# Plain float32 products for the inputs of a state-space stage

## The chip, the cores and the metric

The kernel runs on one core of one Trainium2 chip. Its time is the device time of one execution in microseconds. TensorE (PE) multiplies, PEld is its loading of the stationary operand, VectorE (DVE), ScalarE (ACT) and GpSimd (POOL) work on tiles, and SyncE (SP) issues nearly all transfers.

## The reference

Two layers of a backbone over 512 latent and 256 context tokens of width 1024, all in float32. Layer 0 has a matrix-memory mixer, layer 1 the state-space mixer (Mamba-2, two directions); a mixer of 16384 experts stands behind each. The change concerns the first line of the state-space mixer's preparation, once for the context and once for the latent tokens:

```python
def prep(h):
    z, xbc, dt_raw = jnp.split(h @ w_in, [B_DI, B_DI + B_CONV_CH], axis=-1)   # 1024 x 6208
    xbc = jax.nn.silu(dw_conv(xbc, conv_w, conv_b))
    xs, bm, cm = jnp.split(xbc, [B_DI, B_DI + B_GROUPS * B_STATE], axis=-1)
    dt = softplus(dt_raw + dt_bias)
    ...
```

`w_in` has 2048 columns for the gate z, 2048 for x, 1024 for B, 1024 for C and 64 for dt. Behind it come a convolution over 5 tokens with SiLU, the chunked scan in both directions (chunks of 128 tokens, 32 heads in 8 groups), a gated norm and the output product. The context's state is where the latent scan starts; the context's own output is not needed, since the layer is the last.

## The kernel before

**Products.** TensorE takes a stationary operand of 128 x 128 and a moving one of 128 x up to 512. Most large products of the kernel are made of exact parts: a float32 number is split in hi (a cast to the type float32r) and lo (the rest, again float32r), and `mm3` (L207 to L210) adds three products in PSUM: hi x hi, hi x lo, lo x hi. One "product" below is such a group of three on the same k (128 rows of the contraction) and the same 128 output channels or tokens.

**Weights.** `raw2` (L149) has SP fetch two k of a weight block in one transfer of 128 x 2 x 512 (512 KB) into one of three `raw` tiles. `wpair` (L165) splits each k: ACT casts it to `whi` (L173), DVE subtracts to get `wlo` (L175), with three tiles of each. A block of weights is 8 k x 512 columns.

**The stage.** `ssd_ctx_in` scales the context, transposes it and splits it (`cinh`, `cinl`); this is done within the expert mixer of layer 0, ahead of the stage. `ssd_ctx` multiplies it with six blocks (B twice, x four times): 32 products of 256 columns each. Behind a block come, for each of four channel groups, the convolution (`conv_silu`: pad L399 and cva L401 on ACT, four cva L403 on DVE, tanh L404 on ACT, st L405 on DVE), transposes (L1142), and for x the state updates (`upd_state`: wx and S L1147 on ACT, a product L1155 on PE, S L1161 on DVE). In the middle, `ssd_in` makes the latent input (`inh`, `inl`, L308 to L313 and L185, L186). `dt_prep` (L1097) multiplies by the 64 dt columns, with its weights split too (w8h, w8l).

`ssd_lat` has 12 latent blocks of 32 products of 512 columns: B and C for four groups, x and z (z with tokens as output rows, `tok_block`), then B and C for the other four, with the scan woven in:

```python
weave(scan(0), project_xz(1))
weave(scan(1), project_bc(1), project_xz(2))
weave(scan(2), project_xz(3))
weave(scan(3), itertools.islice(first, DK))    # the output product's first 12 k
```

A scan has 8 steps (4 chunks x 2 groups). A step fetches the decay sums as a broadcast tile `bcs` of 512 KB (L1313, two buffers), works on it on DVE (L1317, L1319, L1326, L1327) and ACT (L1320, L1325), multiplies states (L1331, L1332, PE), multiplies the weights with x (L1343, four products on PE), and sums on DVE (L1338 to L1346).

**What sets the order.** The code above is only the order of writing. When the kernel is built, a scheduler with its own timing model orders the instructions of each engine; on the chip each engine's queue then runs in that fixed order, and an instruction that waits holds all that stands behind it on its engine. SP's transfers are such a queue as well.

## Time and profile before

| | |
|---|---|
| runs | 5936.06, 5928.29, 5920.93 us; median 5928.29 |
| profiled execution | 5929.8 us, its span 5928.0 us |
| PE | 5272.5 us busy, 89%, 25708 products |
| PEld | 4330.6 us, 73% |
| DVE | 4623.1 us, 78% |
| ACT | 2508.2 us, 42% |
| POOL | 1517.6 us, 26% |
| granted TensorE clock, mean | 0.937 |

Busy time is the union of an engine's instructions. A product's record runs from its start until its last result is out, so records of products that follow each other overlap; what a product occupies is read from one start to the next. The granted clock is the share of 2.4 GHz that TensorE had; its two levels are 1.2 and 2.4 GHz, so 0.91 is a mean over time at either. A plain float32 product with both operands float32 has two records, each with a weight load of its own.

### The profile page before, as it was taken

What the parts mean: (1) busy time and instruction counts of PE and PEld (TensorE: products, weight loads), DVE (VectorE), ACT (ScalarE), POOL (GpSimd) and SP (SyncE); (2) the same over time, 40 slices, a digit from 0 to 9 for tenths busy, and PEclk for the clock granted to TensorE, in tenths of its full rate; (3) what the DMA queues carried; (4) which work ended last, traced back from release to release, by engine and by line L of the source; (5) the groups of instructions that cost most, each with busy time, mean ns of one, the idle gap of its engine ahead of it and who ended that gap; (6) DMA issues with size and microseconds to landing.
All of it is one profiled execution on the core that took longest, in us unless ns stands there. A gap on an engine that the chain in (4) does not pass through costs nothing.

```text
span 5928.0 us, 76907 instructions
## 1 busy us (share of the span) xinstructions
PE 5272.5 (89%) x25708; PEld 4330.6 (73%) x25708; DVE 4623.1 (78%) x8960; ACT 2508.2 (42%) x5186; POOL 1517.6 (26%) x1284
## 2 busy tenths in 40 slices
PE   6899999999997875998699999788877998799998
PEld 4688777766663444898578899667666898688997
DVE  6743567877676788999888889767776998788888
ACT  4643454322222333344333333477874344333333
POOL 1300001345544445121033444000001011133442
PEclk8999999999998887998799999899888998799999
DMA  6765555898879987566698999433334357798996
GB/s 211 240 191 156 161 164 163 282 333 303 301 248 320 327 313 254 168 198 213 207 340 315 347 336 332 155 97 96 104 110 125 121 180 250 254 339 321 345 339 234
DMA packets 655799, 1406.96 MB, mean 237 GB/s; under 512 B 62760, under 2 KB 237496, under 8 KB 650920
## 3 DMA queue, kind: packets, MB, share of 16 engines
q1 hardware_dynamic: 507944, 865.11, 44.1%
q0 software_dynamic: 147456, 536.94, 25.7%
q8 instruction: 201, 3.29, 0.2%
q14 instruction: 198, 1.62, 0.1%
HBM read 1278.10 MB, written 123.70 MB: 236 GB/s over the span
## 4 chain that ended last, share of the span: by engine, by line
PE 40%; DVE 13%; DMA 13%; issue 6%; ACT 4%; POOL 1%; DVEq 0%; SPq 0%; ACTq 0%; POOLq 0%
PE mm L208 6%; PE mm L209 6%; PE mm L210 6%; PE sm L210 4%; PE sm L208 4%; PE sm L209 4%; DMA g<-in_v_dram,idv 4%; DMA g<-in_u_dram,idx 3%; DVE wlo L175 2%; DMA bcs<-acD 2%; PE mx L1032 2%; PE mx L210 1%; PE mx L208 1%; PE mx L209 1%; DMA raw<-in_v_dram 1%
## 5 line engine op out<-in xcount | busy, mean ns | idle before, releaser
L173 ACT CAST whi<-raw 128x512 fp32r<-128x512 f32 x2032 | 1227.0, 619 | 1815.4 <-PE mm L209 575.7
L175 DVE TENSOR_TENSOR wlo<-raw,whi 128x512 fp32r<-128x512 f32 x1979 | 1348.3, 695 | 499.8 <-ACT whi L173 488.0
L860 POOL DMA_INDIRECT g<-in_u_dram,idx x512 | 623.4, 1218 | 1465.8 <-PE mx L210 418.0
L860 POOL DMA_INDIRECT g<-in_v_dram,idv x512 | 679.3, 1327 | 888.0 <-DVE acc L878 316.8
L878 DVE SCALAR_TENSOR_TENSOR acc<-g,act,acc 128x1024 f32<-128x1024 f32 x508 | 655.7, 1291 | 156.2 <-DMA g<-in_v_dram,idv 153.6
L867 DVE CUSTOM_DVE_ANT_0 g<-g,xb 128x1024 f32<-128x1024 f32 x512 | 622.4, 1220 | 161.8 <-DMA g<-in_u_dram,idx 160.6
L210 PE MATMUL sm<-pinh,wlo 128*128 128x384 f32 x2048 | 693.1, 342 | 14.8 <-DVE wlo L175 14.2
L208 PE MATMUL sm<-pinh,whi 128*128 128x384 f32 x2048 | 697.1, 340 | 4.3 <-ACT w L977 3.0
L209 PE MATMUL sm<-pinl,whi 128*128 128x384 f32 x2048 | 694.2, 339 | 0.0
L209 PE MATMUL mm<-wlo,wh 128*128 128x512 f32 x1024 | 400.6, 394 | 11.1 <-DVE wlo L175 11.0
L210 PEld LDWEIGHTS sm<-pinh,wlo 128*128 128x128 f32 x2048 | 386.0, 189 | 23.2 <-DVE wlo L175 22.5
L210 PE MATMUL mm<-whi,wl 128*128 128x512 f32 x1024 | 393.8, 391 | 3.2 <-DVE wl L186 3.2
L208 PEld LDWEIGHTS sm<-pinh,whi 128*128 128x128 f32 x2048 | 386.5, 189 | 12.6 <-ACT w L977 5.6
L208 PE MATMUL mm<-whi,wh 128*128 128x512 f32 x1024 | 362.5, 396 | 35.0 <-ACT wh L185 31.0
L209 PEld LDWEIGHTS sm<-pinl,whi 128*128 128x128 f32 x2048 | 386.6, 189 | 5.5
L209 PE MATMUL mm<-xcl,whi 128*128 128x256 f32 (+1 forms) x1024 | 349.2, 346 | 8.9 <-DVE xcl L186 8.9
L210 PE MATMUL mm<-xch,wlo 128*128 128x256 f32 (+1 forms) x1024 | 332.0, 349 | 21.6 <-DVE wlo L175 21.4
L208 PE MATMUL mm<-xch,whi 128*128 128x256 f32 (+1 forms) x1024 | 344.3, 349 | 5.1 <-ACT xch L185 4.0
L208 PE MATMUL mm<-inh,whi 128*128 128x512 f32 (+1 forms) x768 | 285.8, 376 | 11.1 <-ACT cva L401 6.9
L1057 DVE TENSOR_TENSOR w<-w,gtb 128x384 f32<-128x384 f32 x256 | 232.5, 912 | 63.8 <-DMA gtb<-gD 28.6
L209 PE MATMUL mm<-inl,whi 128*128 128x512 f32 (+1 forms) x768 | 279.9, 366 | 0.0
L1032 PE MATMUL mx<-og,oa 128*128 128x128 f16 x1536 | 199.2, 297 | 86.3 <-DVE og L1027 86.2
(478 smaller groups left out, 10947.3 us busy)
## 6 DMA issues: line engine op xcount, KB each, us to landing
raw<-in_uT_dram SPq DMA_DIRECT2D x256, 512.0 KB
raw<-in_v_dram SPq DMA_DIRECT2D x256, 512.0 KB
raw<-in_w_qk_dram SPq DMA_DIRECT2D x128, 512.0 KB
raw<-in_ada_w_dram SPq DMA_DIRECT2D x96, 512.0 KB
raw<-in_w_up_dram SPq DMA_DIRECT2D x96, 512.0 KB
gD<-sg SPq DMA_DIRECT2D x48, 1024.0 KB
gtb<-gD SPq DMA_DIRECT2D x32, 1536.0 KB
raw<-in_s_in_dram SPq DMA_DIRECT2D x72, 512.0 KB
```

Source lines behind the costliest of these rows:

```text
L173: nc.scalar.copy(hi, raw[:, u])
L175: (eng or next(los["eng"])).tensor_tensor(lo, raw[:, u], hi.bitcast(F32), OP.subtract)
L208: nc.tensor.matmul(o, sh, mh, start=start, stop=False)
L209: nc.tensor.matmul(o, sh, ml, start=False, stop=False)
L210: last["pe"] = nc.tensor.matmul(o, sl, mh, start=False, stop=stop)
L860: d = nc.gpsimd.indirect_dma_start(out=g_, out_offset=None, in_=tab, in_offset=bass.IndirectOffsetOnAxis(ap=ix[:, k:k + 1], axis=0))
L867: nc.vector.tensor_tensor_reduce(out=g_, in0=g_, in1=xb, scale=1.0, scalar=0.0, op0=OP.mult, op1=OP.add, accum_out=act[:, k:k + 1])
L878: nc.vector.scalar_tensor_tensor(acc, g_, act[:, k:k + 1], acc, OP.mult, OP.add)
L1032: nc.tensor.matmul(g4[:, k * P:(k + 1) * P], oa[:, f, :, k], og[:, u, :, k], start=u == 0, stop=u == 1)
L1057: nc.vector.tensor_tensor(w, w, gt[0][:, :, j], OP.mult)
```

## The change

The inputs are no longer split. `ssd_ctx_in` and `ssd_in` write one float32 tile each (`cinx`, `inx`), `parts` copies instead of splitting where no lo tile is given, `dt_prep` uses its weights as fetched, and `ch_block` and `tok_block` multiply the fetched weights (`wraws`, the raw tile itself) with it in one plain float32 product in place of three.

```diff
+    def wraws(wt, n, kc):
+
+        for k in range(0, kc, 2):
+            raw = raw2(wt[n, k:k + 2].rearrange("k p c -> p k c"))
+            for u in range(2):
+                yield raw[:, u]
+                tick()
...
+    def parts(hi, lo, s, src):
+
+        if lo is None:
+            nc.scalar.copy(hi[s], src)
+        else:
+            split(hi[s], lo[s], src)
...
+    def ch_whole(o, wt, n, kc, x):
+
+        T = o[0].shape[1]
+        pair = T == CTX
+        for k, w in enumerate(wraws(wt, n, kc)):
+            for c in range(4):
+                last["pe"] = nc.tensor.matmul(o[c], w[:, c * P:(c + 1) * P], x[:, k, :T], start=k == 0 and not pair,
+                                              stop=k == kc - 1 and not (pair and c % 2 == 0))
+            yield
...
-        for _ in ch_steps(o, wt, n, kc, xh, xl, eng):
+        for _ in ch_whole(o, wt, n, kc, xh) if xl is None else ch_steps(o, wt, n, kc, xh, xl, eng):
...
+        if xl is None:
+            for k, w in enumerate(wraws(wt, n, kc)):
+                for t, x in enumerate(o):
+                    last["pe"] = nc.tensor.matmul(x, xh[:, k, t * P:(t + 1) * P], w, start=k == 0, stop=k == kc - 1)
+            return o
...
-                split(xh[s], xl[s], o.rearrange("p (c t) -> p c t", c=4))
+                parts(xh, xl, s, o.rearrange("p (c t) -> p c t", c=4))
...
-            w8h = wq.tile([P, 8, 64], F32R, name="w8h")
-            w8l = wq.tile([P, 8, 64], F32R, name="w8l")
-            split(w8h, w8l, w8)
             for k in range(8):
-                mm3(o[:64, :nt * P], w8h[:, k], w8l[:, k], inh[:, k, :nt * P], inl[:, k, :nt * P], k == 0, k == 7)
+                nc.tensor.matmul(o[:64, :nt * P], w8[:, k], x_in[:, k, :nt * P], start=k == 0, stop=k == 7)
...
-        inh = pool.tile([P, 8, T], F32R, name="inh")
-        inl = pool.tile([P, 8, T], F32R, name="inl")
+        x_in = pool.tile([P, 8, T], F32, name="inx")
...
-        inh = cinp.tile([P, 8, CTX], F32R, tag="cinh", name="cinh", bufs=1)
-        inl = hcp.tile([P, 8, CTX], F32R, tag="h_ctx", name="cinl", bufs=1)
+        x_in = cinp.tile([P, 8, CTX], F32, tag="cinh", name="cinx", bufs=1)
...
-                for c, o in enumerate(ch_block(A["s_in"], 4 + n, 8, inh, inl, T)):
+                for c, o in enumerate(ch_block(A["s_in"], 4 + n, 8, x_in, None, T)):
...
-                for t, o in enumerate(tok_block(A["s_in"], n, 8, inh, inl, T)):
+                for t, o in enumerate(tok_block(A["s_in"], n, 8, x_in, None, T)):
```

The scheduler orders the instructions anew from the context input's transposes on; ahead of these the order is the same on every engine. On POOL nothing moves.

On ACT, in the context part at the first x block, before the change (xst is the transposed x, pad, cva and st the convolution, wx the x scaled by dt, whi the casts):

```order
L1147 ACTIVATE wx<-xst,dt_wst_32170 128x64 x12
L173 CAST whi<-raw 128x512
L404 ACTIVATE st<-cva 128x256
L401 ACTIVATE cva<-mm,c_scb,c_scw 128x256
L399 COPY pad<-mm 128x256
L173 CAST whi<-raw 128x512
L1233 COPY xst<-sm 128x2x128
L173 CAST whi<-raw 128x512
L401 ACTIVATE cva<-mm,c_scb,c_scw 128x256
L173 CAST whi<-raw 128x512
L1233 COPY xst<-sm 128x2x128
```

The same place on ACT after it, with the lines of the changed kernel:

```order
L1174 ACTIVATE wx<-xst,dt_wst_32068 128x64 x6
L1258 COPY xst<-sm 128x2x128
L431 ACTIVATE cva<-mm,c_scb,c_scw 128x256
L434 ACTIVATE st<-cva 128x256
L429 COPY pad<-mm 128x256
L431 ACTIVATE cva<-mm,c_scb,c_scw 128x256
L1258 COPY xst<-sm 128x2x128
L1174 ACTIVATE wx<-xst,dt_wst_32068 128x64 x4
```

The casts are gone from between the steps of the convolution and the scaling.

On PE, at the end of the last block of input products (the fourth z block, within the third scan), before the change (S,cT and xt,m are products of scan steps, wx,btk state updates):

```order
L209 MATMUL mm<-wlo,inh 128x512
L1155 MATMUL sm<-wx,btk 128x256
L210 MATMUL mm<-whi,inl 128x512
L1331 MATMUL mx<-S,cT 128x256
L1332 MATMUL mx<-S,cT 128x256
L1343 MATMUL mx<-xt,m_37438 128x64 x4
L1155 MATMUL sm<-wx,btk 128x256 x2
L1331 MATMUL mx<-S,cT 128x256
L1332 MATMUL mx<-S,cT 128x256
L1343 MATMUL mx<-xt,m_37489 128x64 x4
```

And after it, from the last input products (mm<-raw,inx) on:

```order
L274 MATMUL mm<-raw,inx 128x512 x8
L1182 MATMUL sm<-wx,btk 128x256 x4
L1169 MATMUL sm<-ident,st 128x128 x4
L1357 MATMUL mx<-S,cT 128x256
L1182 MATMUL sm<-wx,btk 128x256
L1356 MATMUL mx<-S_35205,cT 128x256
L1357 MATMUL mx<-S,cT 128x256
L1169 MATMUL sm<-ident,st 128x128 x4
L1368 MATMUL mx<-xt,m_35425 128x64 x4
```

From the last input product to the first product of the output block there are four groups of L1343 before the change, and seven of L1368 after it.

## Rows read from the trace of the kernel before

**Rows 1.** The windows: busy us (x instructions) of each engine, clock, DMA.

```profile
3747.00:3794.00 47.00, 42.52 (x298) 39.12 (x298) 37.77 (x76) 26.07 (x47) 0.00 (x0) 0.91 0.52 165
3794.00:3998.00 204.00, 169.38 (x818) 132.69 (x818) 139.47 (x320) 139.43 (x393) 0.00 (x0) 0.87 0.29 89
3998.00:4056.00 58.00, 53.68 (x255) 43.56 (x254) 36.09 (x64) 42.59 (x122) 0.00 (x0) 1.00 0.30 90
4056.00:4102.00 46.00, 35.74 (x163) 28.25 (x162) 40.96 (x80) 39.34 (x124) 0.00 (x0) 0.93 0.33 98
4102.00:4166.00 64.00, 61.24 (x300) 49.87 (x299) 50.98 (x98) 55.02 (x158) 0.00 (x0) 1.00 0.40 119
4166.00:4230.00 64.00, 47.96 (x198) 37.72 (x196) 54.93 (x107) 50.51 (x161) 0.00 (x0) 0.81 0.32 91
4230.00:4298.00 68.00, 59.57 (x276) 48.49 (x276) 40.41 (x76) 52.52 (x147) 0.00 (x0) 0.95 0.32 103
4298.00:4340.00 42.00, 36.98 (x171) 29.47 (x170) 36.30 (x68) 35.53 (x107) 0.00 (x0) 0.92 0.40 119
```

**Rows 2.** The chain of waits in 3740 to 4350, by line.

```profile
by line: DMA bcs<-acD 10.5%; PE mm L208 8.9%; DVE cva L403 8.6%; PE mm L210 8.4%; PE mm L209 8.2%; ACT wx L1147 5.4%; issue 4.4%; ACT S L1147 4.0%; ACT whi L173 2.4%; DVE wlo L175 2.3%; ACT cva L401 2.2%; DVE bcs L1317 2.0%; ACT pad L399 1.
```

**Rows 3.** The timeline of PE, latent block: start us, us, instruction.

```profile
3943.76 0.39 PE L208 MATMUL mm<-inh,whi 128*128 128x512 f32 x1
...
3944.46 0.40 PE L208 MATMUL mm<-inh,whi 128*128 128x512 f32 x1
```

**Rows 4.** The timeline of PEld, context block.

```profile
3756.85 0.19 PEld L208 LDWEIGHTS mm<-cinh,whi 128*128 128x128 f32 x1
...
3757.20 0.19 PEld L208 LDWEIGHTS mm<-cinh,whi 128*128 128x128 f32 x1
```

**Rows 5.** The timeline of PEld, query-key product of layer 0, idle before in brackets.

```profile
1406.48 0.19 PEld L558 LDWEIGHTS sm<-qk,kc 128*128 128x128 f32 x1 [0.24 <-issue]
1406.91 0.19 PEld L558 LDWEIGHTS sm<-qk,kc 128*128 128x128 f32 x1 [0.24 <-issue]
```

**Rows 6.** Groups of PE: count, busy us, mean ns, idle before.

```profile
L558 PE MATMUL sm<-qk,kc 128*128 128x512 f32 x64 | 29.6, 602 | 0.0
```

**Rows 7.** The timeline of PEld, value product of layer 0.

```profile
1896.32 0.84 PEld L718 LDWEIGHTS mm<-v,pr 128*128 128x128 f32 x4
1897.19 0.40 PEld L717 LDWEIGHTS mm<-v,pr 128*128 128x128 f32 x2
```

**Rows 8.** The windows of L208 alone: PE and PEld busy us, clock, DMA.

```profile
3747.00:3794.00 47.00, 28.20 (x96) 19.56 (x96) 0.91 0.52 165
...
4298.00:4340.00 42.00, 11.87 (x32) 6.46 (x32) 0.92 0.40 119
```

**Rows 9.** Groups of ACT in 3740 to 4350.

```profile
L173 ACT CAST whi<-raw 128x512 fp32r<-128x512 f32 x144 | 87.1, 617 | 54.9 <-PE mm L209 39.4 <-PE mm L210 12.1 <-DVE cva L403 1.4
```

**Rows 10.** Groups of DVE in 3740 to 4350.

```profile
L175 DVE TENSOR_TENSOR wlo<-raw,whi 128x512 fp32r<-128x512 f32 x144 | 97.7, 684 | 55.6 <-ACT whi L173 48.8 <-PE mm L210 6.5
...
L186 DVE TENSOR_TENSOR inl<-sm,inh 128x512 fp32r<-128x512 f32 x8 | 5.5, 686 | 1.3 <-ACT inh L185 1.3
```

**Rows 11.** Who waited for whom in 3740 to 4350: us, times, longest.

```profile
DVE wlo L175 <- ACT whi L173: 48.8, 32, 4.5
ACT whi L173 <- PE mm L209: 39.4, 33, 3.8
DVE bcs L1317 <- DMA bcs<-acD: 37.7, 19, 4.9
```

**Rows 12.** The same of SP's queue in 3740 to 4490.

```profile
SPq L152 <- DVE wlo L175: 209.4, 52, 18.7
```

**Rows 13.** The chain in order of time: start us, us, what.

```profile
4322.69 5.53 DMA bcs<-acD
```

**Rows 14.** The same, fourth scan: the last products of two steps.

```profile
4417.77 1.97 PE mx L1343 x8
...
4452.26 1.94 PE mx L1343 x8
```

More of the change, by code (lines that the diff above doesn't have):

```diff
@@ L1095, in ssd_consts, with dt_prep @@
         sc1.update(dtb=dtb, ar=ar, sd=sd)
-    def dt_prep(pool, sp, inh, inl, nt):
+    def dt_prep(pool, sp, x_in, nt):
         r = {k: pool.tile([P, nt, 64], F32, name=f"dt_{k}{nt}") for k in ("dt", "acs", "eacs", "wst", "eal")}
@@ L1167, in ssd_in @@
         acD = tc.dram_tile([nt, 64, P], F32, name="acD")
-        inh = pool.tile([P, 8, T], F32R, name="inh")
-        inl = pool.tile([P, 8, T], F32R, name="inl")
+        x_in = pool.tile([P, 8, T], F32, name="inx")
         def steps():
             with tc.tile_pool(name="slr", bufs=1, reuse_waits="tile") as q:
-                make_in(q, 1, 0, 0, 1, lambda t, p_: h(t), T, inh, inl)
-            dts = dt_prep(pool, pool, inh, inl, nt)
+                make_in(q, 1, 0, 0, 1, lambda t, p_: h(t), T, x_in, None)
+            dts = dt_prep(pool, pool, x_in, nt)
             dtr = next(dts)
-            yield inh, inl, dtr, acD
+            yield x_in, dtr, acD
             for _ in dts:
@@ L1185, in ssd_in, with ssd_ctx_in @@
         return steps()
-    def ssd_ctx_in(pool, get, hcp, cinp):
+    def ssd_ctx_in(pool, get, cinp):
         ys = [big_g(pool) for _ in range(2)]
@@ L1200, in ssd_ctx_in, with ssd_ctx @@
                 s = (slice(None), slice(half * 4, half * 4 + 4), slice(t * P, (t + 1) * P))
-                split(inh[s], inl[s], o.rearrange("p (c t) -> p c t", c=4))
-        return inh, inl
-    def ssd_ctx(inh, inl, SD, lat, rest):
+                parts(x_in, None, s, o.rearrange("p (c t) -> p c t", c=4))
+        return x_in
+    def ssd_ctx(x_in, SD, lat, rest):
         T, nt = CTX, CTX // P
@@ L1208, in ssd_ctx @@
             with tc.tile_pool(name="scv", bufs=1, reuse_waits="tile") as q:
-                dts = dt_prep(pool, q, inh, inl, nt)
+                dts = dt_prep(pool, q, x_in, nt)
                 for n_, n in enumerate((4, 5, 0, 1, 2, 3)):
@@ L1223, in ssd_ctx @@
                         xs = q.tile([P, nt, 512], F32, tag="xst", name="xst", bufs=2)
-                    for c, o in enumerate(ch_block(A["s_in"], 4 + n, 8, inh, inl, T,
+                    for c, o in enumerate(ch_block(A["s_in"], 4 + n, 8, x_in, None, T,
                                                    nc.vector,
@@ L1242, in ssd_ctx, with ssd_lat @@
         return (*res, lat)
-    def ssd_lat(h, SD, inh, inl, dtr, acD, dts):
+    def ssd_lat(h, SD, x_in, dtr, acD, dts):
         T, nt = LAT, LAT // P
@@ L1267, in project_xz @@
                 zt[n] = q.tile([P, nt, 512], F32, tag="zt", name="zt", bufs=2)
-                for c, o in enumerate(ch_block(A["s_in"], 4 + n, 8, inh, inl, T)):
+                for c, o in enumerate(ch_block(A["s_in"], 4 + n, 8, x_in, None, T)):
                     j = 4 * n + c
@@ L1510, in backbone @@
     modulation(1, MODS[1], mmb)
-    cin, rest = peer_lat(0, hl, pp, lambda: ssd_ctx_in(pp, hc, hcpool, cinp), ppx.close)
+    cin, rest = peer_lat(0, hl, pp, lambda: ssd_ctx_in(pp, hc, cinp), ppx.close)
     next(rest)
@@ L1515, in backbone @@
     with tc.tile_pool(name="sl", bufs=1, reuse_waits="tile") as lp:
-        lat = ssd_ctx(*cin, SD, ssd_in(lp, hl), rest)
+        lat = ssd_ctx(cin, SD, ssd_in(lp, hl), rest)
         hcp.close()
```

## The prediction

> **What bounds the kernel now.** I read the page first: PE is busy 89% of the span, DVE 78%, ACT 42%, so a change that gives PE more work and takes work from ACT and DVE must be judged in its own stage. The stage is short: from the first context product to the last latent one it is 593 us, which the windows cut in eight [rows 1]. PE is busy in 507.1 of them, DVE in 436.9, ACT in 441.0, and PE's clock is granted at 0.91 on average (0.81 to 1.00). No engine is full over the stage, but the stretches differ: in 3998 to 4056 and 4102 to 4166 PE idles 4.3 and 2.8 us at clock 1.00, while in 4166 to 4230 it idles 16.0 us and DVE is busy 54.9 of 64. The first kind is bound by the products, the second by the scan and the convolution on DVE and ACT.
>
> Then the chain of waits over 3740 to 4350 (610 us) [rows 2]: the three passes have 8.9 + 8.4 + 8.2 = 25.5% of it, 156 us; the scan's broadcast (bcs) has 10.5%, 64 us; the two casts that the change removes have 2.4 + 2.3 = 4.7%, 28.7 us. So casts are on the path for a third of the time that either engine spends on them, and the products for less than half of theirs.
>
> **The change part by part.**
>
> *PE, added.* A product of 512 columns is three passes whose starts lie 0.233 apart: from one L208 to the next, three passes on, 0.70 us [rows 3]. One of 256 columns takes 0.35 us [rows 4]. What plain float32 costs is shown by the query-key product of layer 0: its weight loads follow each other in 0.43 us [rows 5], and its 4 heads x 2 key chunks x 4 = 32 products have 64 records [rows 6], two each, so 0.86 us. For 256 columns the value product of the same layer has four records in 0.87 us [rows 7], so 0.435 us a product. The added price is 0.16 us for 512 columns and 0.085 us for 256. There are 12 latent blocks of 32 products and 8 for dt (392), and 6 context blocks of 32 and 8 for dt (200): 392 x 0.16 + 200 x 0.085 = 62.7 + 17.0 = 80 us of PE time.
>
> The Trainium skill prices a pass by itself at N/2.4 + 2.5 ns ("TensorE: Matmul & The Clock Gate", Back-to-back issue gap) and true float32 at four passes ("FP8 and Floating Point Precision", TensorE Precision Notes). By that three passes would cost 0.65 us and the plain product 0.86 us, 0.21 us more instead of 0.16, and with 0.11 us for 256 columns the addition would be an estimated 106 us and the sum below 26 us higher. The trace agrees on the plain product, but its passes of exact parts are 0.233 apart and not 0.216, so the sum goes by the rows.
>
> *How much of it lies in PE's idle time.* The products of a window are the L208 records in it: 96 in the first, then 208 (16 of them dt), 64, 32, 64, 32, 64, 32 (the first and the last of the eight rows stand in [rows 8]). Added against idle, window by window: 8.2 against 4.5; 25.5 against 34.6; 10.2 against 4.3; 5.1 against 10.3; 10.2 against 2.8; 5.1 against 16.0; 10.2 against 8.4; 5.1 against 5.0. Where the addition is larger the window grows by the difference: 3.7 + 5.9 + 7.4 + 1.8 + 0.1 = 18.9 us. In the other three PE waits for something else, and the longer products lie inside that wait.
>
> *ACT and DVE, removed.* 144 casts whi of 617 ns, 87.1 us on ACT [rows 9], and 144 subtractions wlo of 684 ns, 97.7 us on DVE, with 8 for the latent input, 5.5 us [rows 10]; the four for the context input lie in the stage before, where I cost their 2.7 us at nothing since the products of the expert mixer cover them. More than the busy time goes: a cast stands in ACT's queue until PE frees one of three whi buffers, and ACT is held 39.4 us by that (54.9 us in all ahead of casts), while DVE waits 48.8 us for the cast [rows 11]. The change's order on ACT shows what comes forward: the scaling by dt and the convolution, which stood behind casts. How much of this reaches the path? From below the chain's 28.7 us; from above ACT's wait and the latent subtractions, 54.9 + 5.5 + 2 for the two split dt weights = 62 us. A chain names one waiter at a time and is the nearer measure, so I take 28.7.
>
> *Transfers, moved.* There are three raw tiles, each of two k. Before, one came free when both halves were split, and the split could run three k ahead of PE: 12 products, 8.4 us. Now it comes free with PE's last product on it. SP already waits 209.4 us for wlo ahead of raw transfers in this stage and the next stretch [rows 12]. Two tiles stay ahead of PE: 4 k x 4 products x 0.86 = 13.8 us in the latent part, 7 us in the context part, against 5.5 us for a bcs transfer of the same 512 KB [rows 13]. So PE doesn't wait for weights, and I cost this at nothing. What it can cost is a bcs behind a raw that waits longer: DVE waits 37.7 us for bcs now [rows 11], and I let that double at most, 38 us.
>
> *The scan, moved.* In the change's order on PE the last block of products has been put earlier against the scan: seven scan steps (each ends in the L1343 products, L1368 of the change) follow the last input product of the third scan, four did before. A step that nothing covers takes (4452.26 - 4417.77) / 5 = 6.9 us [rows 14]. If the three are simply late, that is 21 us; but while they are out of the projection they free DVE and ACT there. I take 0, with 21 us in the range.
>
> *Sum.* +18.9 - 28.7 = -9.8 us on the profiled 5929.8 us: **5920 us**. The median of the runs shown is 5928.3, 1.5 us under the profiled run.
>
> **Bounds.** From below: if the added 80 us fill PE's 86 us of idle entirely and the clock rises from 0.91 to 1.00 over 593 us (53 us), the stage is 59 us shorter, 5871. From above: all 80 us appear, 6010.
>
> **The rivals.**
>
> *The casts were the true limit (faster).* ACT held behind casts is what delays the scaling, the convolution and so the scan everywhere; then 62 us come back against 18.9: 5929.8 - 43 = 5887. For it: rows 11, and ACT busy 139 of 204 us around the context scan. Against it: the chain gives casts only 4.7%, and PE with its longer products would have to run almost without idle.
>
> *PE in series (slower).* PE's idle time is dependency wait (a product waits for a scan step, the step for the product), and longer products only push both. Then the 156 us of products on the chain grow by 0.16/0.70, +36 us, and the casts' slack turns into waits for PE: 5965. It decides if PE still idles some 80 us in the same windows after. For it: the products are already the largest thing on the chain, and full stretches have 2.8 to 8.4 us of room for 8 to 10. Against it: in 4166 to 4230 and around 3794 to 3998 idle time is larger than the addition and stands beside a busy DVE.
>
> *SP's queue (slower).* Raw transfers held until PE is through stand ahead of bcs transfers: 5920 + 38 = 5958. For it: rows 12. Against it: SP's order has been made anew with the change.
>
> *Nothing moves.* The scan with its two bcs buffers sets the pace and both sides are hidden: 5930.
>
> **How the numbers follow.** The forecast has 0.42, with its own range 5900 to 5942 (the scan's 21 us at the top); the casts' rival 0.22, PE in series 0.16, SP 0.10, nothing 0.10. A change under 0.3%, 18 us, can't be told from none: that is 5912 to 5948. Of the forecast 0.12 lies under it and 0.30 within. Faster: 0.12 + 0.22 = 0.34. Same: 0.30 + 0.10 = 0.40. Slower: 0.16 + 0.10 = 0.26. The range 5880 to 5972 takes in the casts' rival and PE in series, and leaves out the ends at 5871 and 6010.
>
> **What would show it.** Products with inx: two records each, 0.43 us apart (512 columns). No whi or wlo in the stage, and ACT's idle ahead of wx and cva smaller. PE's idle in the eight stretches down from 86 us to some 30, with the clock up from 0.91; if it stays near 80, PE is in series. DVE's wait for bcs near 38 us; near 75 it is SP's queue. The stretch up to 3998 should shrink, and the two full ones grow by 6 to 7 us. A third scan with a longer tail after its last product shows the moved steps. Wrong altogether would be a stage that changes by more than 60 us, or time that moves ahead of the context input's transposes, where the order is the same.

## The result, and the profile after

| | before | after |
|---|---|---|
| median of 6 runs each | 5935.88 us | 5969.15 us |
| ratio, 95% interval | | 1.0056 [1.0036, 1.0076] |
| profiled execution, its span | 5929.8, 5928.0 us | 5968.8, 5967.0 us |
| first context product to last latent product | 589.6 us | 596.8 us |
| from there to the output block's first product ("the tail") | 26.1 us | 61.4 us |
| from there to the end | 1564.7 us | 1563.2 us |

The change makes the kernel slower by 33 us. The forecast was 5920 us, with 0.40 on no change and 0.26 on slower; the time lies inside the range of 5880 to 5972, on the wrong side of the forecast. Differences below are (ratio - 1) x 5932 us unless they are called a stage of a trace.

The windows of after, cut at the same events as [rows 1]; columns as there:

```profile
3745.00:3792.00 47.00, 47.00 (x202) 37.66 (x203) 27.83 (x70) 17.12 (x35) 0.00 (x0) 0.94 0.51 161
3792.00:3984.00 192.00, 175.46 (x594) 104.17 (x593) 99.39 (x245) 107.56 (x330) 0.00 (x0) 0.93 0.31 87
3984.00:4040.00 56.00, 53.11 (x150) 25.44 (x149) 23.88 (x42) 21.61 (x54) 0.00 (x0) 0.97 0.27 86
4040.00:4100.00 60.00, 58.37 (x187) 31.43 (x186) 35.91 (x71) 43.56 (x145) 0.00 (x0) 0.99 0.36 94
4100.00:4170.00 70.00, 63.45 (x186) 33.01 (x186) 38.00 (x76) 36.69 (x106) 0.00 (x0) 0.94 0.31 96
4170.00:4230.00 60.00, 57.17 (x162) 28.48 (x161) 43.20 (x84) 41.33 (x125) 0.00 (x0) 0.97 0.28 84
4230.00:4298.00 68.00, 64.04 (x207) 34.86 (x206) 37.69 (x67) 32.03 (x106) 0.00 (x0) 0.97 0.41 107
4298.00:4342.00 44.00, 36.04 (x111) 20.33 (x110) 21.09 (x41) 31.57 (x87) 0.00 (x0) 0.77 0.30 84
```

The stretch up to the last latent product and the tail, of before and then of after:

```profile
3747.60:4337.20 589.60, 503.69 (x2453) 406.80 (x2453) 435.32 (x884) 437.66 (x1239) 0.00 (x0) 0.91 0.34 102
4337.20:4363.30 26.10, 15.21 (x57) 11.64 (x55) 17.06 (x34) 18.48 (x66) 0.00 (x0) 0.67 0.32 85
3745.50:4342.30 596.80, 554.44 (x1792) 315.38 (x1792) 326.80 (x691) 331.28 (x982) 0.00 (x0) 0.94 0.33 96
4342.30:4403.70 61.40, 32.92 (x126) 24.24 (x124) 41.01 (x78) 49.88 (x181) 0.00 (x0) 0.63 0.33 89
```

Read the first engine column (PE) against the length: up to the last product PE idles 42 us, where it idled 86 [rows 1], and but for the last 44 us the clock is 0.93 to 0.99. DVE and ACT, busy for 74% of the time up to the last product before (435 and 438 of 589.6 us), have 55% (327 and 331 of 596.8). So PE is nearly full, the two others have air, and still the end comes later: in the tail PE has work for half of the time.

What each product costs came out as priced. The timeline of PE in a latent block, and of PEld (weight loads) in a context block:

```profile
4004.78 2.31 PE L274 MATMUL mm<-raw,inx 128*128 128x512 f32 x5
4006.93 1.04 PE L1169 MATMUL sm<-ident,st 128*128 128x128 f32 x8
```

```profile
3763.94 2.13 PEld L251 LDWEIGHTS mm<-cinx,raw 128*128 128x128 f32 x10
```

Five records start within 2.15 us, 0.43 each, and a product has two [rows 6]. The context's ten loads take 2.13 us, 0.43 for the two of a product [rows 7].

The chain by line over 3740 to 4350, as [rows 2]:

```profile
by line: PE mm L251 32.6%; DMA bcs<-acD 16.5%; PE mm L274 7.9%; DVE cva L433 4.5%; DVE bcs L1342 3.4%; PE sm L1182 2.5%; ACT bcs L1350 2.1%; PE sm L1137 2.0%; ACT wx L1174 1.9%; ACT m L1350 1.7%; issue 1.5%; DVE m L1352 1.5%; DVE m L1351 1.
```

The products go from 25.5% to 40.5%, the casts are gone, and the broadcast goes from 10.5% to 16.5%. Who waited in the same stretch (as [rows 11]), and in SP's queue up to 4490 (as [rows 12]):

```profile
DVE bcs L1342 <- DMA bcs<-acD: 80.8, 20, 6.3
```

```profile
SPq L152 <- PE mm L251: 183.3, 44, 16.5
SPq L1338 <- DVE m L1352: 166.7, 27, 15.5
SPq L152 <- PE mm L274: 75.0, 14, 14.2
```

DVE's wait for bcs has doubled. On SP, raw transfers (L152) now wait for PE's products, and bcs transfers (L1338), as before, for the operation on DVE that frees their buffer (L1352). In the tail the bcs transfer has 49.0% of the chain, more than anything else. The chain there in order of time, what ends SP's longest gap (read below), one period whole, and of the others the transfer:

```profile
4363.14 0.42 DVE S L1188
4363.56 0.61 DVE m L1351
4364.20 0.57 DVE m L1352
4364.92 5.14 DMA bcs<-acD
...
4373.85 5.27 DMA bcs<-acD
...
4382.50 5.06 DMA bcs<-acD
4387.58 1.22 DVE bcs L1342
4388.81 0.60 DVE m L1351
4389.41 0.60 DVE bcs L1344
4390.01 0.34 DVE sx L1363
4390.35 0.61 DVE m L1352
4391.02 5.34 DMA bcs<-acD
...
4399.83 4.76 DMA bcs<-acD
```

Scan steps that no product covers run as a loop: a transfer, four or five operations on DVE, of which the last (L1352) frees a bcs buffer, then the next transfer. This L1352 is that of the step before: counted in DVE's order, the 23rd L1352 of the 32 stands behind the 24th L1342, which waits for the 24th transfer, and the 25th transfer needs the buffer that it frees. So two buffers give no transfer ahead here. Four periods take 34.9 us, 8.7 each (6.9 in [rows 14]). SP's queue in this stretch also has a gap of 19 us with no bcs, between 4345.57 and 4364.92, in which it holds transfers of states and of finished tiles. The chain leaves it by a state update on DVE (S L1188), which waits for PE's products of states, and L1352 behind it:

```profile
4345.57 0.37 SPq L1338 DMA_DIRECT2D bcs<-acD  x1
4351.53 5.64 SPq L1324 DMA_DIRECT2D S<-SD  x2
4358.32 6.31 SPq L1405 DMA_DIRECT2D st<-yTD  x3
4364.92 17.93 SPq L1338 DMA_DIRECT2D bcs<-acD  x3
```

So the loss is seen in the tail. Whether it is made there, and by what (products that cost more, casts that gave nothing, held transfers, or the order), the trace doesn't tell.

### The profile page after: what moved, and what is told of

Read it like the earlier page. It is cut to its first block, busy times and chain, and to the rows that moved or that the text cites. A ratio compares the mean times of both kernels' runs of the same rounds, so it can differ in the third digit from the quotient of the medians.

```text
span 5967.0 us, 75232 instructions
## 1 busy us (share of the span) xinstructions
PE 5338.9 (89%) x25116; PEld 4248.3 (71%) x25116; DVE 4535.5 (76%) x8802; ACT 2433.1 (41%) x5040; POOL 1543.0 (26%) x1284
## 4 chain that ended last, share of the span: by engine, by line
PE 38%; DMA 15%; DVE 12%; issue 8%; ACT 3%; POOL 1%; SPq 0%; DVEq 0%; POOLq 0%; ACTq 0%
DMA g<-in_v_dram,idv 5%; PE sm L225 4%; PE sm L223 4%; PE sm L224 4%; PE mm L224 4%; PE mm L223 4%; PE mm L225 4%; DMA g<-in_u_dram,idx 4%; PE mm L251 3%; DMA bcs<-acD 3%; DVE wlo L175 2%; PE mx L225 1%; PE mx L224 1%; PE mx L223 1%; DVE g L897 1%
## 5 line engine op out<-in xcount | busy, mean ns | idle before, releaser
L173 ACT CAST whi<-raw 128x512 fp32r<-128x512 f32 x1888 | 1140.2, 620 | 1740.8 <-PE mm L224 529.5
L175 DVE TENSOR_TENSOR wlo<-raw,whi 128x512 fp32r<-128x512 f32 x1835 | 1249.9, 696 | 431.7 <-ACT whi L173 417.7
L890 POOL DMA_INDIRECT g<-in_u_dram,idx x512 | 639.9, 1250 | 1440.2 <-PE mx L225 420.2
L225 PE MATMUL sm<-pinh,wlo 128*128 128x384 f32 x2048 | 691.7, 342 | 14.6 <-DVE wlo L175 14.5
L193 ACT CAST wh<-w 128x384 fp32r<-128x384 f32 x256 | 131.7, 514 | 326.6 <-DVE w L1087 228.1
L1062 PEld LDWEIGHTS <-oa 128*128 128x128 bf16 x1536 | 168.0, 121 | 113.0 <-DVE og L1057 97.7
```

Source lines behind the costliest of these rows:

```text
L173: nc.scalar.copy(hi, raw[:, u])
L175: (eng or next(los["eng"])).tensor_tensor(lo, raw[:, u], hi.bitcast(F32), OP.subtract)
L193: nc.scalar.copy(hi, src)
L225: last["pe"] = nc.tensor.matmul(o, sl, mh, start=False, stop=stop)
L890: d = nc.gpsimd.indirect_dma_start(out=g_, out_offset=None, in_=tab, in_offset=bass.IndirectOffsetOnAxis(ap=ix[:, k:k + 1], axis=0))
L1062: nc.tensor.matmul(g4[:, k * P:(k + 1) * P], oa[:, f, :, k], og[:, u, :, k], start=u == 0, stop=u == 1)
```

## The experiments

Theory 1: the new order on PE puts the scan behind the products, and its steps run uncovered. Theory 2: the products' price, in series. Theory 3: SP holds bcs behind raw transfers. Two came up on the way: theory 4, that once PE's idle time is used up all of its extra time shows, and theory 5, that the raw tiles which PE now holds until its last product on them make the loss. Where a kernel's order matters, this table has it (the kernels are described below, where they are measured): how many of the 384 latent products stand on PE ahead of the steps of the second scan and of the third (counted in each order), and the stage by its trace, in us.

| kernel | ahead of the second scan's 8 steps | third's first 4 | steps behind the last product | to the last product | tail |
|---|---|---|---|---|---|
| before | 244 256 256 257 258 265 272 288 | 332 352 361 376 | 4 | 589.6 | 26.1 |
| after | 267 310 317 324 334 343 352 360 | 376 384 384 384 | 7 | 596.8 | 61.4 |
| four passes, no casts | 242 264 268 272 283 290 298 304 | 352 365 374 383 | 4 | 592.4 | 26.0 |
| order of four passes | 254 280 281 282 286 298 300 310 | 352 375 380 383 | 4 | 599.3 | 30.0 |
| second scan tied | 256 264 265 266 268 268 280 288 | 352 384 384 384 | 7 | 611.1 | 46.5 |
| third scan tied | 267 310 317 324 334 343 352 352 | 352 375 380 383 | 4 | 627.5 | 27.2 |
| order of before | 251 256 256 260 262 274 284 288 | 347 352 360 370 | 4 | 633.6 | 30.9 |
| held raw tiles | 245 264 271 272 279 288 297 304 | 354 384 384 384 | 7 | 563.2 | 42.8 |
| order of held raw tiles | 255 264 266 266 274 280 288 296 | 362 384 384 384 | 7 | 584.7 | 55.7 |
| blocks tied | 224 224 224 224 256 256 256 256 | 352 352 352 352 | 4 | 674.1 | 20.1 |

**One part alone: context, latent.** Either part gets back `x_lo`, `mm3` and its casts.

```diff
-        x_in = pool.tile([P, 8, T], F32, name="inx")
+        x_in = pool.tile([P, 8, T], F32R, name="inh")
+        x_lo = pool.tile([P, 8, T], F32R, name="inl")
```

> Only the context part of the stage uses plain products; the latent part keeps three passes of exact parts. Theory 1 (the loss is the third scan, which falls behind the longer products on PE and then runs seven steps uncovered): the context part keeps its 22 us and the scan keeps a short tail (three steps follow the last input product in the order), so 15 to 25 us faster than before, about 5912. Theory 2 (the price of the products themselves in series): 200 products of 256 columns at 0.085 us are 17 us more, so 5 to 17 us slower than before. Theory 3 (transfers held behind the raw tiles): no change within 5 us, since the scan's broadcasts run in the latent part.

Measured: 5910.77 us, 0.9963 [0.9951, 0.9975], 22 us faster than before. To the last product and the tail:

```profile
3739.70:4320.00 580.30, 512.22 (x2265) 406.21 (x2265) 411.10 (x843) 416.55 (x1207) 0.00 (x0) 0.92 0.35 105
4320.00:4337.40 17.40, 10.53 (x45) 7.91 (x43) 16.01 (x32) 15.63 (x53) 0.00 (x0) 0.72 0.33 101
```

The context's products end 123.5 us after their start (139.8 before), and the tail is short. It is the only version here that keeps all of the numbers and is faster than before.

The other way round:

```diff
-        x_in = cinp.tile([P, 8, CTX], F32, tag="cinh", name="cinx", bufs=1)
+        x_in = cinp.tile([P, 8, CTX], F32R, tag="cinh", name="cinh", bufs=1)
+        x_lo = hcp.tile([P, 8, CTX], F32R, tag="h_ctx", name="cinl", bufs=1)
```

> Only the latent part uses plain products; the context part keeps three passes. Theory 1: the tail stays seven steps long and the context's gain is gone, so 45 to 60 us slower than before, about 5985 to 5995, and some 20 us slower than the full change. Theory 2: 392 products at 0.16 us on the chain for half of their time, about 30 us slower than before and 5 to 10 us faster than the full change. Theory 3: 33 us slower, like the full change.

Measured: 5981.78 us, 1.0091 [1.0073, 1.0108], 54 us slower than before, with a tail of 61.2 us. Both runs are as theory 1 had it and not as theory 2 or 3. The context part gains 22 us, and the latent part loses 54. Its order of products and scan steps is that of after.

**The price without the casts, and the casts at the plain price.** The first kernel reads one weight tile that is cast once (`wfx`) in three passes; the second makes whi and wlo in `wraws` for nobody.

```diff
+                w_, x_ = w[:, c * P:(c + 1) * P], x[:, k, :T]
+                mm3(o[c], w_, w_, x_, x_, k == 0 and not pair, ...)
```

```diff
+                hi = wp.tile([P, 512], F32R, tag="whi", name="whi", bufs=3)
+                nc.scalar.copy(hi, raw[:, u])
+                lo = wp.tile([P, 512], F32R, tag="wlo", name="wlo", bufs=3)
+                nc.vector.tensor_tensor(lo, raw[:, u], hi.bitcast(F32), OP.subtract)
```

> The full change's casts (none in the stage) at the PE price of before: each product is three passes of exact-part type, 0.70 us for 512 columns. It leaves out the numbers: the passes read one weight tile that is cast once, and the input has no low part, so the raw tiles are fetched and never read. Eight scan steps follow the last input product in its order. Theory 1: PE gets 80 us back and the products end earlier, but the uncovered tail stays; the stage is 30 to 40 us shorter ahead of the tail and the tail is as long as after or a step longer: 0 to 15 us faster than before, and 30 to 45 us faster than the full change, with the stretch from the last input product to the output block still about 60 us. Theory 2: all of the loss is PE's price, so without it the casts' 28.7 us come through whole: about 29 us faster than before, and that stretch is back near 26 us.

Measured: 5893.95 us, 0.9931 [0.9913, 0.9949], 41 us faster than before. Its two stretches:

```profile
3741.80:4254.90 513.10, 465.34 (x2373) 386.10 (x2373) 321.98 (x687) 320.91 (x952) 0.00 (x0) 0.93 0.33 107
4254.90:4327.60 72.70, 36.15 (x137) 27.06 (x135) 44.55 (x84) 57.03 (x209) 0.00 (x0) 0.66 0.27 73
```

The products are through 76 us earlier than before, and 47 of these are given back in a tail of 72.7 us. Theory 2 is nearer with its total of 29 us, but not with its reason: the tail, which it had near 26 us, is as long with cheap products. Theory 1 had the tail and undersized the gain ahead of it. The stage of the trace, tail included, is 30 us shorter than before.

> The full change with the casts made again beside it: each weight half is cast on ACT and subtracted on DVE into tiles that nobody reads, 87 us on ACT and 98 us on DVE, and the raw tiles also wait for them. Theory 1 (PE sets the pace of the stage, the scan on DVE and ACT sets the tail, and the freed cast time bought nothing on PE's path): 10 to 40 us slower than the full change, since casts now only take time from the scan. Theory 2 (casts were 28.7 us of the path and are given back): about 29 us slower than the full change, with PE's idle time in the stage 30 us larger. If the casts are hidden altogether: within 10 us of the full change.

Measured: 5969.4 us, 1.0056 [1.0041, 1.0071]: the same as the full change. Groups of DVE and ACT in its stage:

```profile
L192 DVE TENSOR_TENSOR wlo<-raw,whi 128x512 fp32r<-128x512 f32 x138 | 91.7, 688 | 65.0 <-ACT whi L190 64.6
L190 ACT CAST whi<-raw 128x512 fp32r<-128x512 f32 x138 | 78.9, 616 | 94.8 <-DMA raw<-in_s_in_dram 84.0 <-DVE wlo L192 7.1 <-DVE pad L432 3.8
```

171 us of casts are back and the time stays (within some 15 us, by the two intervals): ACT now waits for raw tiles ahead of them, not for PE. Theories 1 and 2 both expected a cost; the third sentence had the total. The trace shows a sum of two parts, though. The context's products take 142.3 us from first to last, 23 more than in after (119.7), so there the casts do cost. From the first latent product to the output block it is 520 us against 534 in after, with an order made anew (the second scan behind 275, 300, 300, 312 ... 352 products). That the casts are free in after's order isn't shown.

**Buffers, and a coarse tie.** Four bcs buffers; then the first product of each latent block tied on PE behind the scan step written ahead of it; both; and three more raw tiles.

```diff
-                        bcs = q.tile([P, 2, 4, P], F32, tag="bcs", name="bcs", bufs=2)
+                        bcs = q.tile([P, 2, 4, P], F32, tag="bcs", name="bcs", bufs=4)
```

```diff
+                if k == 0:
+                    behind(last["pe"])
```

```diff
+            if "raw" in los and k % 4 == 0:
+                raw = los["raw"].tile([P, 2, 512], F32, tag="rawq", name="rawq", bufs=3)
```

> The full change with four bcs buffers instead of two (they fit in the space that the input's low part left). Theory 1 (in the tail each step's broadcast starts only when the buffer of two steps before is freed, so transfer, subtraction and multiplication go in series at 8.7 us a step): the transfers run ahead, the seven steps of the third scan and some of the fourth's come at the pace of DVE, some 5 us a step, 20 to 40 us faster than the full change, so about 5940. Rival (the steps are paced by the work on DVE and ACT itself): within 8 us of the full change, DVE's wait for bcs moves to another wait.

Measured: 5963.28 us, 1.0039 [1.0027, 1.0051], some 10 us faster than the full change by the ratios (the intervals overlap). The tail is still 60.9 us: its transfers still start about 8 us apart, and SP has its gap. The chain in it:

```profile
4372.38 1.23 DVE bcs L1342
...
4373.94 0.60 DVE m L1352
4374.57 4.87 DMA bcs<-acD
```

The loop is the same, only deeper. Counted in DVE's order, this is the 24th L1342 and the 21st L1352: the scheduler has put the operation that frees a buffer three steps behind, and the 25th transfer waits for it as before. So the run didn't undo the loop, and what the tail would be without it isn't shown.

> The full change with the order on PE tied again: the first product of each latent block stands behind the last scan step that the code writes ahead of it, so that four scan steps follow the last input product as before, and not seven. Theory 1 (the order that puts products ahead of the scan costs the tail): the last input product comes 5 to 15 us later, the stretch from it to the output block falls from 61 to some 35 us, in all 10 to 20 us faster than the full change, about 5952. Rival (PE is full, and order only exchanges one wait for another): within 8 us of the full change, with PE's idle time moved from the tail into the stage.

Measured: 6006.22 us, 1.0110 [1.0093, 1.0126], 65 us slower than before. The two stretches:

```profile
3742.30:4416.40 674.10, 583.89 (x1861) 333.86 (x1861) 348.49 (x737) 368.40 (x1116) 0.00 (x0) 0.90 0.32 90
4416.40:4436.50 20.10, 13.63 (x56) 11.06 (x54) 15.17 (x30) 12.53 (x42) 0.00 (x0) 0.75 0.41 120
```

The tail went, as expected, but PE idles 90 us ahead of it. The rival had idle time moving there; that the kernel would be 32 us slower than the full change neither had. The miss taught that the number of steps behind the last product is not the thing by itself.

> Both edits: four bcs buffers and the tied order. Theory 1: what is left of the loss is PE's time alone, so the third scan keeps up with the products and the tail is under 30 us: 30 to 45 us faster than the full change, 5925 to 5940. Rival: no better than the better of the two edits by itself.

Measured: 6007.91 us, 1.0110 [1.0094, 1.0125]: as the rival had it.

> The full change with six raw tiles for the latent blocks instead of three, so that raw transfers leave SP's queue earlier. Theory 3 (SP holds bcs transfers behind raw transfers that wait for PE): DVE's wait for bcs falls from 81 us towards 38, and 15 to 40 us of the loss come back. Theories 1 and 2 (PE's time and the scan's own loop): within 8 us of the full change, and the tail after the last input product stays at about 60 us.

Measured: 5991.35 us, 1.0097 [1.0079, 1.0115]. More raw tiles made it 24 us slower than the full change, with eight steps behind the last product in an order made anew and a tail of 78.5 us. DVE's wait for bcs doesn't fall (104 us in 3740 to 4420, 98 in after). All three theories missed. It doesn't test theory 3: the first latent product comes 52 us behind the last context product (4.5 in after), since it waits for the first of the new tiles, whose transfer stands on SP behind 13 transfers of the context's states. Once begun, the latent products take 430 us to the last one against 473 in after, so the late start and the longer tail are what made it slower.

**PE's price.** A fourth pass, low part by low part, in 11 of 16 products or in all, first in the kernel before and then in the one without casts.

```diff
+        if next(cnt) % 16 < 11:
+            nc.tensor.matmul(o, sl, ml, start=False, stop=False)
```

> The kernel before, casts and all, with a fourth pass (low part by low part) in 11 of 16 input products: 192 x 11/16 x 0.117 + 384 x 11/16 x 0.233 = 77 us more on PE, about what the plain products cost, and nothing else changed; four scan steps follow the last input product as before. Theory 4 (PE's time is the limit of the stage as soon as its idle time is used up; of 80 us more some 41 lie in idle time that the casts leave, the rest shows): 33 to 40 us slower than before, the loss of the full change without its edits. Theory 1 (the order of the scan made the loss): the order stays, so at most 15 us slower. The forecast's sum by windows: 19 us slower.

Measured: 5961.97 us, 1.0041 [1.0027, 1.0055], 24 us slower. Ahead of the tail:

```profile
3762.60:4379.20 616.60, 563.45 (x2850) 464.97 (x2850) 436.35 (x884) 437.36 (x1240) 0.00 (x0) 0.94 0.33 98
```

In every product, with the condition gone:

> The same with the fourth pass in every input product: 112 us more on PE. Theory 4: idle time is used up, so all that comes beyond the first 77 us shows, 112 - 41 = 71 us slower than before, 65 to 78. If the products are a fixed share of the path (156 of some 412 us of product time): 43 us slower here, and 29 us in the smaller dose.

Measured: 5988.7 us, 1.0075 [1.0057, 1.0093], 44 us slower. 77 us of PE time cost 24, 112 cost 44: 0.31 and 0.40 of the price. Theory 4's 71 falls outside the interval of 34 to 55, and the fixed share's 29 and 43 fit; the window sum's 19 lies within the first run's 16 to 33. The tail stays at 25 to 28 us in both, with four steps behind the last product. The order isn't quite that of before, which the expectation took as given: the third scan's first step stands behind 352 products in both, not 332. PE's price alone doesn't make the tail.

The same pass in the kernel without casts:

> The kernel without casts at three passes per product, as measured above, with a fourth pass in 11 of 16 products: 77 us more on PE, so PE's time is that of the full change, but the order has four scan steps behind the last input product and not seven. It leaves out the numbers as that kernel does. Theory 4: without casts nothing else fills the stage, so 65 to 77 us slower than without the fourth pass, and within 10 us of the full change: 5960 to 5975. Theory 1: the short tail keeps the loss away: some 30 us faster than the full change.

Measured: 5935.26 us, 0.9993 [0.9981, 1.0004], no different from before: 37 us slower than without the fourth pass, and 37 faster than the full change. Its stretches:

```profile
3741.60:4334.00 592.40, 554.65 (x2850) 464.06 (x2850) 344.35 (x732) 360.12 (x1086) 0.00 (x0) 0.94 0.32 98
4334.00:4360.00 26.00, 14.57 (x57) 11.06 (x55) 19.64 (x38) 20.55 (x75) 0.00 (x0) 0.64 0.32 75
```

Set against after's own two stretches above, PE is busy 554 us up to the last product in either, there are no casts in either, and the tail differs by 35 us. That is the loss, and theory 4 falls. Left were the order, the raw tiles that PE holds only in after, and the plain products themselves.

**The full change in another order.** Each scan step's L1368 product is tied on PE ahead of the latent product whose number `AT` gives; no other line does anything new. The scheduler orders the other engines anew along with it (on ACT about a quarter of the stage's instructions stand in another place), and products of higher numbers may still stand ahead of a step, so the steps come to stand where the table has them.

```diff
+    AT = [[160, 171, 178, 185, 192, 203, 207, 213], [242, 264, 268, 272, 283, 290, 298, 304], [352, 365, 374, 383]]
...
+            tc.add_manual_dep(prods[i].ins, late[i].ins.name, mybir.DependencyInfo(
+                mybir.DependencyClass.NoSync, mybir.DependencyReason.DATA), reason="behind the scan step")
```

> The full change, all its products plain, with each scan step of the first three scans tied in PE's order ahead of the same product as in the kernel of four passes without casts (for the second scan after 242, 264, 268 ... 304 of 384 latent products, where the full change has 267, 310, 317 ... 360). Theory 1 (the order made 34 us of the loss): 25 to 40 us faster than the full change, no different from before, 5925 to 5945. Theory 5 (raw tiles that PE holds make the loss): within 10 us of the full change. If the tied order makes PE wait as the coarser one did: slower than the full change.

Measured: 5929.74 us, 0.9998 [0.9988, 1.0009]. The loss is gone, 34 us faster than the full change, with the same products and the same tiles held. Theory 5 falls with it. Its profiled execution is 27 us above its median; some 9 us of the difference to after's trace lie behind the stage and 8 ahead of it, so the stage is what to read:

```profile
3753.40:4352.70 599.30, 560.04 (x1862) 321.83 (x1862) 345.59 (x728) 358.93 (x1082) 0.00 (x0) 0.95 0.34 100
4352.70:4382.70 30.00, 16.48 (x57) 12.38 (x55) 21.73 (x43) 22.10 (x81) 0.00 (x0) 0.57 0.33 91
```

As long as after up to the last product, and a tail of half the length. No different from before is a balance: the context's products take 116.9 us from first to last (139.8 before), and from the first latent product to the output block it is 507.8 us (475.8 before, 534.0 in after). So in this execution the latent part still loses, and plain products in the context alone are 21 us faster than this by the ratios.

In the order of before the numbers of the second scan are these (the first and third scan's are that kernel's too):

```diff
+    AT = [[...], [244, 256, 256, 257, 258, 265, 272, 288], [332, 352, 361, 376]]
```

> The same with the order of before (second scan after 244, 256, 256, 257 ... 288 products). Theory 1: 15 to 40 us faster than the full change; as this order was made for other durations PE may wait some 10 us more than in the other one. Theory 5: within 10 us of the full change.

Measured: 5959.21 us, 1.0050 [1.0034, 1.0065], 4 us faster than the full change by the ratios, which the intervals don't tell from none. The order of before holds PE: 633.6 us to the last product, with a tail of 30.9. This order, made for other durations, is no remedy.

With four bcs buffers (`bufs=4`) beside the tied order of four passes:

> The tied order of the four-pass kernel and four bcs buffers. Theory 1: both gains, 35 to 45 us faster than the full change, 5925 to 5935, so a little faster than before or the same. Theory 5: no more than the 6 us that four buffers alone gave.

Measured: 5930.11 us, 0.9997 [0.9987, 1.0008]. No more than the order alone.

The four-pass kernel with a plain product on the raw tile as the last of every four (`tok_block` likewise):

```diff
+                if c == 3:
+                    last["pe"] = nc.tensor.matmul(o[c], raw[:, c * P:(c + 1) * P], x[:, k, :T].bitcast(F32), ...)
+                    continue
```

> The kernel of four passes without casts, in which the last of four products of each k is a plain one that reads the raw tile, so that PE holds raw tiles as in the full change; PE's time stays that of the full change within 3 us. It leaves out the numbers like that kernel. Its order on PE is made anew and has seven steps after the last product, like the full change. Theories 1 and 5 both expect the loss back, 5960 to 5975; if it stays near 5935, neither the order nor the held tiles made it, and the plain products themselves are the cause.

Measured: 5911.34 us, 0.9962 [0.9947, 0.9977]. All expectations missed: raw tiles held, PE's price paid, seven steps behind the last product, and 23 us faster than before (10 us of it in the stage of its trace).

```profile
3750.30:4313.50 563.20, 542.00 (x2552) 418.29 (x2552) 333.75 (x709) 345.99 (x1034) 0.00 (x0) 0.96 0.34 103
4313.50:4356.30 42.80, 24.64 (x110) 19.19 (x108) 31.39 (x61) 35.40 (x130) 0.00 (x0) 0.73 0.40 113
```

Seven steps behind the last product don't by themselves make a loss. Its second scan stands after 245, 264, 271 ... 304 products, early like that of four passes; PE idles 21 us up to the last product.

**Which place it is.** The second scan alone, the order of the kernel above, the third scan alone:

```diff
+    AT = [[], [242, 264, 268, 272, 283, 290, 298, 304]]
```

> The full change with only the second scan's eight steps tied ahead of products 242 to 304; they then stand after 256, 264, 265 ... 288 of 384 latent products, and not after 267, 310, 317 ... 360. The third scan is free and keeps seven steps after the last product. Theory 1a (the place of the second scan made the loss): 25 to 40 us faster than the full change, 5930 to 5945, with the stretch from the last product to the output block 15 us or more shorter though it has the same steps. Theory 1b (the seven steps made it): within 10 us of the full change.

Measured: 5962.62 us, 1.0055 [1.0041, 1.0068]: no gain.

```profile
3750.20:4361.30 611.10, 555.41 (x1807) 315.33 (x1807) 334.48 (x708) 346.25 (x1035) 0.00 (x0) 0.94 0.32 96
```

The tail is 15 us shorter, the products 14 us later. The steps came to stand earlier than in the order of four passes (the last after 288 products, there 310), so this isn't that order's second scan by itself.

```diff
+    AT = [[160, 172, 180, 186, 192, 204, 209, 215], [245, 264, 271, 272, 279, 288, 297, 304], [354]]
```

> The full change with the scan steps tied ahead of the products at which the kernel with held raw tiles has them (second scan after 245, 264, 271 ... 304, third scan's first after 354). Theory 1a: like the order of four passes, 5925 to 5940, or down to 5911 if that kernel's whole gain lies in the place of its scan steps on PE. Theory 1b: within 10 us of the full change.

Measured: 5947.09 us, 1.0030 [1.0017, 1.0042], 15 us faster than the full change: half of the loss, in an order with an early second scan and seven steps at the end; neither theory had it. The tail stays at 55.7 us, and most of the gain lies ahead of the last product. The other kernel's 5911 isn't reached, so what makes that one fast is not in these places alone.

```diff
+    AT = [[], [], [352, 365, 374, 383]]
```

> The full change with only the third scan tied: its first four steps stand ahead of products 352, 365, 374 and 383, so that four steps follow the last product, and the second scan is left free, but has to stand ahead of the third. Theory 1b (the uncovered steps made the loss): 25 to 40 us faster than the full change, 5930 to 5945. Theory 1c (both places together are needed, since a third scan tied early waits for a second one that runs late): within 10 us of the full change or slower, with PE's idle time moved ahead of the last product.

Measured: 5966.4 us, 1.0060 [1.0039, 1.0081]: no gain.

```profile
3723.60:4351.10 627.50, 567.70 (x1864) 327.76 (x1864) 349.26 (x733) 362.76 (x1095) 0.00 (x0) 0.93 0.33 96
```

The tail is 34 us shorter, and the products 31 us later: a third scan tied early waits for the second, which still runs late, as theory 1c had it. All three scans tied are worth 34 us, the second or the third alone nothing. The first scan was never tied alone, nor left free where the other two were tied: in after and in the two kernels with one scan tied its steps stand after 160 182 187 192 203 211 219 224 products, in the order of four passes after 160 178 185 190 192 203 211 219 and in that of held raw tiles after 160 181 186 190 192 204 212 220. The orders that gained have its second half earlier too, and how much of the 34 us is its share no run tells.

## Why the prediction was wrong

**The step that failed is "The scan, moved", taken at 0.** It looked at the last block only: seven steps behind the last product, not four, three times 6.9 us. What the order had moved was far more of the scan: step 2 of the second scan stood behind 310 latent products and not 256, so by an estimate from the price per product 54 x 0.86 us = 46 us more of PE's queue lay ahead of it. In the traces that step's products start 422 us after the first context product before, 489 after, and 452 in the tied order. The full change in an order with the steps earlier is 34 us faster (0.9998 against 1.0056), as much as the whole net loss. So the step belonged in the sum with 34 us, not 0, and its 21 us at the top were too few. The hope written beside the 0, that the steps "free DVE and ACT" in the projection, paid nothing: both engines are busy there for 55% of the time, and an order that puts steps back is faster.

**PE's addition, +18.9.** With the casts kept, in an order with the same short tail, 77 us of PE time cost 24 us [16, 33]. The windows took 61 of 80 us as hidden, the run 53 of 77. The step holds.

**The casts, -28.7.** Without them, at three passes, the kernel was 41 us faster [30, 52], 30 of them in the stage; the term was somewhat small and inside its bounds of 28.7 to 62. With plain products, casts put back cost 23 us in the context and nothing in the total, in an order of their own. The value of a term depended on the order that came with it. One reading ahead of it is off: "a third of the time" sets both casts' share of the chain against one engine's time; each by itself has about a sixth (14.6 of 87.1 us, 14.0 of 97.7).

**The sum, -9.8.** The kernel with both terms, no casts and 77 us more on PE, measured -4 us [-11, +2] with an order that suits it, and the change itself in the tied order -1. The two terms fit together. What the change really came with was a third term of 34 us.

**The transfers, at nothing.** PE waits 4.5 us for raw tiles in after, so that part holds. DVE's wait for bcs doubled to 80.8 us, which the prediction's list would have read as SP's queue. But the same wait stands in the tail, where no raw transfer of the stage is left, and two kernels that hold raw tiles were fast. That the doubling is the late scan's own loop fits this and isn't shown by itself.

**The rivals.** PE in series gave 5965, 4 us from the median, for the wrong reason: its condition was that PE still idles some 80 us, and it idles 42. Its 36 of 80 us, a share of 0.45, is a little more than the two doses of a fourth pass showed (0.31 and 0.40). That the time lies inside the range at all is luck: the top of the range was put there for this rival. The casts' rival had the context right: plain there and exact parts in the latent part is 22 us faster.

**What stays open.** Why the scheduler puts the second scan later after the change isn't shown; only the orders it made are. That the order made the loss is shown; which steps of it, and whether their place on PE does it or the orders of DVE, ACT and SP that come with the ties, isn't. Nor is it shown why the kernel with held raw tiles is 18 us faster by the ratios than the one of four passes at the same work: its orders on all engines differ.

## What to carry to other kernels

When a scheduler makes the order anew, compare the place of every waiting step against the work ahead of it, not only the last one, and price the shift in the time of what now stands ahead: here 54 products. Too early costs as well: tied by blocks, the steps left PE idle for 90 us up to the last product, against 42. Tie such places and run again before a change is called slow; one change gave 0.9998 and 1.0110 by ties alone. A change that trades one engine's time for another's may pay in one part only: in the context, where the casts held the products, it was worth 22 us.

## What the runs showed of the hardware

Of TensorE's extra time 0.31 and 0.40 showed while the casts were there (24 of 77 us, 44 of 112), although it is the busiest engine. The granted clock up to the last product, a mean over time at either of its levels, was 0.91 before, with PE busy for 85% of that stretch, and 0.94 in both doses and in the full change, with PE busy for 91 to 93%. PE's busy time up to there grew by 51 us in after, where 80 us were added at the rate of the rows. How much of the difference is the clock's no run separates. In the tails shown, with PE busy for half to two thirds of the time, it was 0.57 to 0.75.

More buffers didn't let transfers run ahead: with two and with four, the operation that frees a buffer stood in DVE's fixed order behind one that waits for a later transfer, and transfers in the tail started about 8 us apart.
